# The last 1024 output columns as seven half products, with weight sums built in DRAM

## The chip, the cores and the metric

The kernel runs on one core of a Trainium2 chip. The metric is the device time of one execution in microseconds. A core has a matrix engine (TensorE, PE in the profile), a vector engine (DVE), a scalar engine (ACT), GpSimd (POOL) and a queue engine that issues transfers (SP); 16 DMA engines move the data. Matrix products leave their results in PSUM, in banks of 512 float32 columns per partition.

## The reference

One layer of a hybrid decoder block on 512 rows of 2048 features, in float32. A normalised input is projected to 5120 columns, which feed three groups of heads: a state space model (1024 output features), differential attention (512) and cross attention to a memory (512). Their concatenated outputs go through one square output projection, whose rows are normalised and added to the input:

```python
mix = jnp.concatenate([y_s, y_d, y_x], axis=-1) @ w_out[l]     # (512 x 2048) @ (2048 x 2048)
x = x + rmsnorm(mix, norm_post[l])                             # mean of squares over all 2048 columns of a row
```

The change concerns this product and what follows it. Everything before it stays, but for the shape of two buffers.

## The kernel before, in words

All products are made at float32 precision from two halves of each factor: `split` and `parts` make a rounded copy `hi` (ACT) and the rest `lo` (DVE), and `mm3` multiplies hi by hi, hi by lo and lo by hi, three matmuls into the same PSUM bank.

The matrix engine's work is a list, `chunks`. A chunk is 512 KB of weights, 128 partitions of 1024 numbers, and a function that issues its matmuls in four units. The loop over `chunks` loads the raw weights some chunks ahead (`load`, tile `raw`, two buffers), splits them two chunks ahead (`parts`, tiles `whi` and `wlo`, three buffers each) and runs the units. Vector and scalar work hangs on quarter chunks: `at_slot(n, f)` calls f after a unit of chunk n. Matmuls are kept in the order in which they are written. On the other engines and in SP's queue a planner may put an instruction that is ready ahead of an earlier one that is not; the marks that `parts` leaves keep vector and scalar instructions behind the split before them. Engines work their queues in order.

The stages are: input projection, state space scan (to chunk `S1`), its gate (`w_glu`, `S1` to `S2`), the remaining projections and cross attention (`S2` to `S3`), differential attention (`S3` to `S4`), and from `S4` the output projection. S4 begins at about 617 us.

The output projection has the weights `w_out_b`, in 4 blocks of 512 columns with 8 chunks each; a chunk holds two slabs of 128 rows of the weight matrix and 512 columns. A block takes, in each chunk, 4 row tiles of 128 rows x 2 slabs x 3 matmuls of 512 columns: 24 per chunk, 192 per block. The factor from the left, kept in SBUF as hi and lo, is `ys` (8 slabs, from `out_open`), `yd` (4) and `yx` (4). Blocks 0 to 2 are made by `add_rows`, four banks `ps_mm` for the four row tiles. `out_evac` then takes a bank: ACT sums the squares of its row (`ojk`, sums in `fin["ss"]`), DVE multiplies by the norm's weights `gpost` into `mix`, which stays in SBUF.

Block 3 is cut: its first four chunks run like the others, over five `pieces`: row tiles 0 to 2, and row tile 3 in two halves of 256 columns, the second half in a bank of its own (`ps_s`). The weights of its last four chunks are all split beforehand (`load_last`, tiles `last4` to `last7`), and so the rest runs piece by piece: a row tile is finished, and while the next one is multiplied, its mean of squares is made (DVE, power -1/2 on POOL), and x plus the scaled mix is written out by DVE (`xres`, `xraw`: two instructions of 1024 columns) and stored. Only the second half of row tile 3 has no matmuls to hide behind. x is loaded by `load_last` into its own buffers.

Of the kernel before, what the change touches and what calls it, by code (L numbers as in the profile page):

```python
# [10 lines left out]
F32 = mybir.dt.float32  # L11
# [8 lines left out]
P = 128  # L20
# [34 lines left out]
def tile_hybrid_block(ctx: ExitStack, tc: tile.TileContext, a: dict, out: bass.AP):  # L55
# [39 lines left out]
    def mm(*args, **kw):  # L95
        pin(pe.matmul(*args, **kw))  # L96
# [1 line left out]
    def transpose(o, i):  # L98
        pin(pe.transpose(o, i, ident))  # L99

    def mm3(o, lh, ll, rh, rl, start, stop):
        mm(o, lh, rh, start=start, stop=False)
        mm(o, lh, rl, start=False, stop=False)
        mm(o, ll, rh, start=False, stop=stop)

    def split(hi, lo, x):
        s.copy(hi, x)
        v.tensor_tensor(lo, x, hi, ALU.subtract)

    def load(src, pieces=1, beside=()):  # L110
        raw = wp.tile([P, 1024], F32, tag="raw", name="raw", bufs=2)
# [45 lines left out]
    def rsqrt_mean(dst, ssq, n):  # L157
        v.tensor_scalar(dst, ssq, 1.0 / n, EPS, ALU.mult, ALU.add)
        g.tensor_tensor(dst, dst, neghalf.to_broadcast([P, dst.shape[-1]]), ALU.pow)
# [35 lines left out]
    def at_slot(n, f):  # L195
        side.setdefault(round(4 * n) + 3, []).append(f)
# [550 lines left out]
    S1 = len(chunks)  # L747
    ge = {}
    gestack, xstack, atstack = ExitStack(), ExitStack(), ExitStack()
    yx, yd = [], []  # L750

    def ge_open():
        s5stack.close()
        ydxp = right_pool(ctx, "ydxp")
        for lst, nm in ((yx, "yx"), (yd, "yd")):
            for h in range(4):
                lst.append((ydxp.tile([P, SEQ], F32R, name=f"{nm}hi{h}"), ydxp.tile([P, SEQ], F32R, name=f"{nm}lo{h}")))
# [226 lines left out]


    S4 = len(chunks)
    fin = {}
    ys = []
    order = [6, 7, 0, 1, 2, 3, 4, 5]

    def out_open():
        hp.__exit__(None, None, None)
        ysp = ctx.enter_context(tc.tile_pool(name="ysp", bufs=1, reuse_waits="tile"))
        for j in range(8):
            ys.append((ysp.tile([P, SEQ], F32R, name=f"yshi{j}"), ysp.tile([P, SEQ], F32R, name=f"yslo{j}")))
# [12 lines left out]

    def y_rows(k, ts_):
# [3 lines left out]
    def out_evac(tt, acc, c0, i, then=None):  # L1013
        w = acc.shape[-1]
        jk = fin["p"].tile([P, 512], F32, tag="jk", name="ojk", bufs=2)
        s.activation(jk[:, :w], acc, AF.Square, accum_out=fin["ss"][:, tt, i:i + 1])
        if then:
            then()
        v.tensor_tensor(fin["mix"][tt][:, c0:c0 + w], acc, fin["g"][:, c0:c0 + w], ALU.mult)

    for blk in range(3):
        add_rows(a["w_out_b"][blk], NT, y_rows, order, lambda tt, acc, blk=blk: out_evac(tt, acc, blk * 512, blk))


    pieces = [(tt, c0, w) for tt, c0, w in ((0, 0, 512), (1, 0, 512), (2, 0, 512), (3, 0, 256), (3, 256, 256))]
    lastacc = {}

    def out_piece(i, ci_, wh, wl):
        tt, c0, w = pieces[i]
        if ci_ == 0:  # L1030
            lastacc[i] = psum("mm" if i < 4 else "s")
        for kk in range(2):
            lh, ll = y_rows(2 * order[ci_] + kk, slice(tt * P, (tt + 1) * P))
            sl = slice(kk * 512 + c0, kk * 512 + c0 + w)
            mm3(lastacc[i][:, :w], lh, ll, wh[:, sl], wl[:, sl], ci_ == 0 and kk == 0, ci_ == 7 and kk == 1)

    for ci_ in range(4):
        def f(wh, wl, ci_=ci_):
            for i in range(5):
                out_piece(i, ci_, wh, wl)  # L1040
                if i != 3:
                    yield
        chunks.append((a["w_out_b"][3, order[ci_]], f))
# [4 lines left out]
    def load_last():
        for ci_ in range(4, 8):
            hl = tuple(fin["w"].tile([P, 1024], F32R, name=f"last{ci_}{x}") for x in "hl")  # L1050
            split(*hl, load(a["w_out_b"][3, order[ci_]]))
            last.append(hl)
        for tt in range(NT):
            for i in range(2):
                if tt < 3:
                    xr = fin["p"].tile([P, 1024], F32, tag="xres", name="xres", bufs=4)
                else:
                    xr = wp.tile([P, 1024], F32, tag="raw", name="xraw", bufs=2)
                sy.dma_start(xr, a["x"][tt * P:(tt + 1) * P, i * 1024:(i + 1) * 1024])
                fin["x", tt, i] = xr  # L1060

    at_slot(S4 + 26, load_last)


    for i in range(9):
# [4 lines left out]
    h_pair(2)  # L1070
    sy.dma_start(cst, a["cst"])
    for n, (_, f) in enumerate(chunks):
        while len(raws) <= min(n + 2 if n < 9 else n + 3, len(chunks) - 1):
            raws.append(load(chunks[len(raws)][0]))
        ahead = n + 1 if n < 9 else n + 2
        while len(ready) <= min(ahead, len(chunks) - 1):
            ready.append(parts(raws[len(ready)], mark=n >= 9))
        units = f(*ready[n])
        for i in range(4):
            next(units, None)  # L1080
            for e in side.get(4 * n + i, []):
                e()

    for i, (tt, c0, w) in enumerate(pieces):
        for ci_ in range(4, 8):
            out_piece(i, ci_, *last[ci_ - 4])
        if i == 4:
            pre = fin["p"].tile([P, 1], F32, name="pre")
            v.tensor_reduce(pre, fin["ss"][:, tt, 0:4], AX.X, ALU.add)
            v.tensor_scalar(pre, pre, 1.0 / D, EPS, ALU.mult, ALU.add)  # L1090
        sr = fin["p"].tile([P, 1], F32, tag="sr", name="sr", bufs=4)

        def scale(i=i, tt=tt, sr=sr):
            if i < 3:
                v.tensor_reduce(sr, fin["ss"][:, tt, 0:4], AX.X, ALU.add)
                rsqrt_mean(sr, sr, D)
            else:
                v.tensor_scalar(sr, fin["ss"][:, tt, 4:5], 1.0 / D, pre, ALU.mult, ALU.add)
                g.tensor_tensor(sr, sr, neghalf, ALU.pow)

        out_evac(tt, lastacc[i][:, :w], 1536 + c0, 3 if i < 4 else 4, scale if i != 3 else None)
        if i == 3:
            continue
        widths = (1024, 1024) if i < 3 else (256, 512, 256, 512, 512)
# [93 lines left out]
```

## Time and profile before

| | |
|---|---|
| median of 3 runs | 815.49 us (811.62 to 815.84) |
| the profiled execution, its own time | 815.97 us |
| its span, first to last instruction | 813.9 us |
| granted TensorE clock, mean | 0.994 |
| TensorE busy | 794.4 us, 98% of the span |
| VectorE busy | 545.2 us, 67% |
| ScalarE busy | 358.9 us, 44% |
| GpSimd busy | 28.3 us, 3% |
| bytes moved by DMA | 131.59 MB, 162 GB/s in the mean |

Busy times are of one engine and overlap between engines. A matmul's own duration overlaps with that of the next, so the pace of matmuls is read from the distance of their starts. A row of a group gives total busy time, mean ns of one, and after the bar the idle time of the engine ahead of it with what ended it. Queues of transfers appear as SPq. In a timeline the first number is the start from the beginning of the span, the second the duration.

### The profile page before, as it was taken

What the parts mean: (1) busy time and instruction counts of PE and PEld (TensorE: products, weight loads), DVE (VectorE), ACT (ScalarE), POOL (GpSimd) and SP (SyncE); (2) the same over time, 40 slices, a digit from 0 to 9 for tenths busy, and PEclk for the clock granted to TensorE, in tenths of its full rate; (3) what the DMA queues carried; (4) which work ended last, traced back from release to release, by engine and by line L of the source; (5) the groups of instructions that cost most, each with busy time, mean ns of one, the idle gap of its engine ahead of it and who ended that gap; (6) DMA issues with size and microseconds to landing.
All of it is one profiled execution on the core that took longest, in us unless ns stands there. A gap on an engine that the chain in (4) does not pass through costs nothing.

```text
span 813.9 us, 10924 instructions
## 1 busy us (share of the span) xinstructions
PE 794.4 (98%) x4030; PEld 663.2 (81%) x4030; DVE 545.2 (67%) x1033; ACT 358.9 (44%) x593; POOL 28.3 (3%) x42
## 2 busy tenths in 40 slices
PE   8999999899999999999999999999999999999996
PEld 6877788788878888888888888888888888888885
DVE  4599878648998899847885544668888833232335
ACT  4654433334445545334734533446667532132311
POOL 0000000010000000000000000000100110000000
PEclk9999999999999999999999999999999999999999
DMA  7977767783655555357564322232224345322326
GB/s 245 351 270 255 255 208 243 250 228 89 189 151 158 150 160 159 116 153 272 175 204 166 100 92 91 78 104 78 78 78 141 96 159 175 104 83 99 109 99 258
DMA packets 60357, 131.59 MB, mean 162 GB/s; under 512 B 12688, under 2 KB 26128, under 8 KB 59408
## 3 DMA queue, kind: packets, MB, share of 16 engines
q1 hardware_dynamic: 60304, 130.91, 49.8%
q8 instruction: 31, 0.51, 0.3%
q14 instruction: 22, 0.18, 0.1%
HBM read 109.52 MB, written 21.36 MB: 161 GB/s over the span
## 4 chain that ended last, share of the span: by engine, by line
PE 82%; DVE 8%; DMA 4%; ACT 2%; issue 2%; SPq 1%; POOL 0%; DVEq 0%; POOLq 0%; ACTq 0%
PE ps_mm L96 71%; PE ps_s L96 7%; PE ps_t L96 3%; DMA raw<-in_w_in_a_dram 2%; DVE wlo L71 2%; PE ps_t L99 1%; DVE ra L71 1%; SPq L71 1%; DMA rows<-in_x_dram 1%; DMA par<-in_par_dram 1%; ACT whi L71 1%; DVE sm L71 1%; DVE x L71 1%; ACT cs L71 1%; DVE cs L71 0%
## 5 line engine op out<-in xcount | busy, mean ns | idle before, releaser
L71 DVE TENSOR_TENSOR wlo<-raw,whi 128x1024 fp32r<-128x1024 f32 (+1 forms) x135 | 161.7, 1198 | 155.2 <-ACT whi L71 154.2
L71 ACT CAST whi<-raw 128x1024 fp32r<-128x1024 f32 (+1 forms) x135 | 138.9, 1029 | 258.4 <-PE ps_mm L96 161.4
L96 PE MATMUL ps_mm<-hhi,whi 128*128 128x512 f32 x512 | 203.0, 396 | 2.8 <-DVE ut L71 1.5
L96 PE MATMUL ps_mm<-hlo,whi 128*128 128x512 f32 x512 | 200.6, 392 | 0.8 <-DVE hlo L71 0.8
L96 PE MATMUL ps_mm<-hhi,wlo 128*128 128x512 f32 x512 | 200.2, 391 | 0.0
L96 PEld LDWEIGHTS ps_mm<-hhi,whi 128*128 128x128 f32 x512 | 96.7, 189 | 24.8 <-ACT hhi L71 2.0
L96 PEld LDWEIGHTS ps_mm<-hhi,wlo 128*128 128x128 f32 x512 | 96.6, 189 | 20.7 <-DVE wlo L71 0.2
L96 PEld LDWEIGHTS ps_mm<-hlo,whi 128*128 128x128 f32 x512 | 96.6, 189 | 20.4 <-DVE hlo L71 1.4
L96 PE MATMUL ps_mm<-whi,hhi 128*128 128x512 f32 x128 | 50.0, 390 | 0.0
L96 PE MATMUL ps_mm<-whi,hlo 128*128 128x512 f32 x128 | 49.9, 390 | 0.0
L96 PE MATMUL ps_mm<-wlo,hhi 128*128 128x512 f32 x128 | 49.9, 389 | 0.0
L96 PE MATMUL ps_mm<-whi,yshi 128*128 128x512 f32 (+1 forms) x112 | 43.9, 392 | 0.0
L96 PE MATMUL ps_mm<-wlo,yshi 128*128 128x512 f32 (+1 forms) x112 | 43.3, 387 | 0.0
L96 PE MATMUL ps_mm<-whi,yslo 128*128 128x512 f32 (+1 forms) x112 | 43.3, 386 | 0.0
L96 PEld LDWEIGHTS ps_mm<-whi,hlo 128*128 128x128 f32 x128 | 24.0, 188 | 5.1
L96 PEld LDWEIGHTS ps_mm<-wlo,hhi 128*128 128x128 f32 x128 | 24.0, 188 | 4.8
L96 PEld LDWEIGHTS ps_mm<-whi,hhi 128*128 128x128 f32 x128 | 24.0, 188 | 4.7
L71 DVE TENSOR_TENSOR x<-ra 64x512 f32<-64x512 f32 x32 | 26.3, 822 | 0.8
L71 ACT ACTIVATE pr<-sm,nm 128x128 f32<-128x128 f32 (+3 forms) x32 | 18.0, 564 | 18.8 <-DVE nm L71 18.6
L96 PE MATMUL ps_mm<-gehi,whi 128*128 128x512 f32 x64 | 25.2, 394 | 0.0
L96 PE MATMUL ps_mm<-gehi,wlo 128*128 128x512 f32 x64 | 25.1, 392 | 0.0
L96 PE MATMUL ps_mm<-whi,yxhi 128*128 128x512 f32 (+1 forms) x64 | 24.9, 389 | 0.0
(323 smaller groups left out, 1383.6 us busy)
## 6 DMA issues: line engine op xcount, KB each, us to landing
raw<-in_w_in_a_dram SPq DMA_DIRECT2D x63, 512.0 KB, 3.5
raw<-in_w_out_b_dram SPq DMA_DIRECT2D x32, 512.0 KB, 3.3
raw<-in_w_in_b_dram SPq DMA_DIRECT2D x16, 512.0 KB, 3.3
sp<-sp_dr SPq DMA_DIRECT2D x8, 576.0 KB, 4.6
rows<-in_x_dram SPq DMA_DIRECT2D x4, 1024.0 KB, 7.7
raw<-in_w_kv_a_dram SPq DMA_DIRECT2D x8, 512.0 KB, 3.4
raw<-in_w_kv_b_dram SPq DMA_DIRECT2D x8, 512.0 KB, 4.4
raw<-in_w_glu_a_dram SPq DMA_DIRECT2D x8, 512.0 KB, 4.5
```

The source lines that it names most:

```text
L71: r = f(*args, **kw)
L96: pin(pe.matmul(*args, **kw))
L99: pin(pe.transpose(o, i, ident))
```

## The change

The output matrix's last 1024 columns are seen as 2 x 2 blocks. With Y the left factor (512 x 2048) cut into A11, A21 (rows 0 to 255 and 256 to 511, first 1024 features) and A12, A22 (the last 1024 features), and W the last 1024 columns of the weights cut into four blocks of 1024 x 512, the result needs 8 half products of 256 x 1024 x 512. One level of Strassen's method (in a form with shared sums) makes it from seven: A11, A12 and A22 and four sums of blocks (n1 to n4), each times a block of W or a sum of blocks (t1, T2, T3, T4).

- Blocks 0 and 1 of the output are made as before. Their `mix` goes to DRAM (`mix_dr`, eight stores of 256 KB) and is read back near the end (`load_mix`).
- `sum_steps`: the sums of weight blocks are built in DRAM. For each of four sums and each of its four chunks GpSimd's queue issues a copy of one block's chunk and later a DMA that adds another block's chunk to it: 32 transfers of 512 KB, one every 1.125 chunks from S1 + 1 on. The chunks are then loaded like any weights.
- The sums of blocks of Y are made on chip. `out_open` subtracts rows 256 to 511 of each slab of ys from rows 0 to 255 (`n3f`, 8 DVE instructions of 128x256); `fin_open` splits it to n3; `comb_n24` and `comb_n1` make n2, n4 and n1 in S4 + 7.75 to S4 + 14.75, in halves of 128x1024: two or three DVE additions and a split each.
- From S5 = S4 + 16 on come six products of 4 chunks, in the order A11 times a block, n3 times T3, A12 times a block, n2 times T2, A22 times T4, n1 times t1. A chunk now serves 2 row tiles: 12 matmuls. A11, n2 and n1 go on top of each other in the two banks `ps_t`, n3 and A22 in two banks `ps_mm`, A12 in `ps_s`. At the end of a product ACT copies the partial sum to SBUF (`keep`), or DVE adds the kept one to the bank, and the row sums of squares and the multiplication by `gpost` follow (`c11`, `c21`, `c22` with `out_c`).
- The seventh product, n4, has its four weight chunks split beforehand (`load_last`, into the tiles of ys) and runs as row tile 0, then row tile 1 in two halves of 256 columns, all on the two banks `ps_t`. Residuals (`residual`): row tiles 2 and 3 are written for the time of n4's row tile 0, row tile 0 after it, row tile 1 last.
- Raw weights have two further buffers (`late_raw`, tag nt) for odd chunks after S5, and are loaded up to five chunks ahead. x loads into the tiles of yx and yd, mix into those of n2 and n1, c12 and the kept sums into those of n2, n3 and n3f.

```diff
-        jk = fin["p"].tile([P, 512], F32, tag="jk", name="ojk", bufs=2)
-        v.tensor_tensor(fin["mix"][tt][:, c0:c0 + w], acc, fin["g"][:, c0:c0 + w], ALU.mult)
-    for blk in range(3):
+            v.tensor_tensor(fin["n3f"][:, j], yr[:, 0:256], yr[:, 256:512], ALU.subtract)
...
+    def comb_n24(k):
+        f_ = fin["n3f"][:, k:k + 4]
+        a12, a22 = half2(k)
+        for n, (h_, l_) in (("n2", a22), ("n4", a12)):
+            v.scalar_tensor_tensor(f_, f_, -1.0, h_, ALU.mult, ALU.subtract)
+            v.tensor_tensor(f_, f_, l_, ALU.subtract)
+            split4(fin[n], k, f_)
+            yield
...
+    def sum_steps():
+        for dst, first, second in (("T3", (1, 2), (2, 2)), ("t1", (1, 1), (1, 2)), ("T2", "T3", (1, 1)), ("T4", "T2", (2, 1))):
+            for c in range(4):
+                g.dma_start(sums[dst][c], sums[first][c] if isinstance(first, str) else block(*first, c))
+                yield
+            for c in range(4):
+                g.dma_start(sums[dst][c], block(*second, c), accum_op=ALU.add, max_dma_last_dim=4096)
+                yield
+    for i in range(32):
+        at_slot(S1 + 1 + 1.125 * i, lambda: next(sum_iter))
...
+    def out_evac(tt, acc, blk):
+        square(acc, tt, blk)
+        cs_ = slice(blk * 512, (blk + 1) * 512)
+        mx = fin["p"].tile([P, 512], F32, tag="mx", name="omx", bufs=3)
+        v.tensor_tensor(mx, acc, fin["g"][:, cs_], ALU.mult)
+        sy.dma_start(mix_dr[tt][:, cs_], mx)
+    for blk in range(2):
...
+    def out_c(c_, tt, col, sign=1.0):
+        w = c_.shape[-1]
+        square(c_, tt, 2 if col < 1536 else 3 + (col > 1536))
+        v.scalar_tensor_tensor(c_, c_, sign, fin["g"][:, col:col + w], ALU.mult, ALU.mult)
+    def c22(i, acc):
+        c_ = tile4("ysp", *KC)[:, 2 + i]
+        v.tensor_tensor(c_, acc, fin["pq"][:, 2 + i], ALU.add)
+        out_c(c_, 2 + i, 1536, -1.0)
...
+    product("A11", w_of(1, 1), "t", True, keep(KA, 0))
+    product("n3", s_of("T3"), "mm", True, keep(KA, 1))
+    product("A12", w_of(2, 1), "s", True, c11)
+    product("n2", s_of("T2"), "t", False, keep(KB, 0))
+    product("A22", s_of("T4"), "mm", False, c21)
+    product("n1", s_of("t1"), "t", False, c22)
...
+    for i, tt in enumerate((2, 3, 0, 1)):
+        at_slot(S5 + 20.25 + 0.5 * i, lambda tt=tt: load_x(tt))
+    at_slot(S5 + 19, lambda: load_mix(0))
+    for ci_ in range(4):
+        at_slot(S5 + 18.75 + ci_, lambda ci_=ci_: load_last(ci_))
...
-        while len(raws) <= min(n + 2 if n < 9 else n + 3, len(chunks) - 1):
-            raws.append(load(chunks[len(raws)][0]))
+        while len(raws) <= min(n + 2 if n < 9 else n + 3 if n < S5 - 2 else n + 5, len(chunks) - 1):
+            m = len(raws)
+            raws.append(load(chunks[m][0], raw=late_raw() if m > S5 and m % 2 else None))
...
+    load_mix(1)
+    acc = last_product(0, 0, 512)
+    for tt in (2, 3):
+        residual(tt, row_scale(tt), (1024, 512, 512), (fin["c2"][:, tt - 2], fin["c2"][:, tt]))
+    c12_evac(0, acc, 0)
+    acc = last_product(1, 0, 256)
+    residual(0, row_scale(0), (1024, 512, 512), (fin["m11"][:, 2], c12[:, 0]))
+    c12_evac(1, acc, 0)
+    acc = last_product(1, 256, 256)
+    pre = fin["p"].tile([P, 1], F32, name="pre")
+    v.tensor_reduce(pre, fin["ss"][:, 1, 0:4], AX.X, ALU.add)
+    v.tensor_scalar(pre, pre, 1.0 / D, EPS, ALU.mult, ALU.add)
+    square(acc, 1, 4)
+    sr = fin["p"].tile([P, 1], F32, tag="sr", name="sr", bufs=4)
+    v.tensor_scalar(sr, fin["ss"][:, 1, 4:5], 1.0 / D, pre, ALU.mult, ALU.add)
+    g.tensor_tensor(sr, sr, neghalf, ALU.pow)
+    v.scalar_tensor_tensor(c12[:, 1, 256:], acc, -1.0, fin["g"][:, 1792:], ALU.mult, ALU.mult)
+    residual(1, sr, (256, 256, 512, 512, 512), (fin["m11"][:, 3], c12[:, 1]))
```

More of the change, by code (lines that the diff above doesn't have):

```diff
@@ L108, in split, with load @@
         v.tensor_tensor(lo, x, hi, ALU.subtract)
-    def load(src, pieces=1, beside=()):
-        raw = wp.tile([P, 1024], F32, tag="raw", name="raw", bufs=2)
+    def load(src, pieces=1, beside=(), raw=None):
+        raw = wp.tile([P, 1024], F32, tag="raw", name="raw", bufs=2) if raw is None else raw
         w = 1024 // pieces
@@ L749, in tile_hybrid_block @@
     gestack, xstack, atstack = ExitStack(), ExitStack(), ExitStack()
-    yx, yd = [], []
+    yx, yd, fin = [], [], {}
     def ge_open():
@@ L1025, in tile_hybrid_block @@
[L1025 to L1043, printed above, removed]
+    def square(x, tt, i):
+        jk = fin["p"].tile([P, 512], F32, tag="jk", name="ojk")
+        s.activation(jk[:, :x.shape[-1]], x, AF.Square, accum_out=fin["ss"][:, tt, i:i + 1])
+    mix_dr = [dr.tile([P, 1024], F32, name=f"mix_dr{tt}") for tt in range(NT)]
@@ L1048, in load_last @@
[L1048 to L1060, printed above, removed]
@@ L1062, in tile_hybrid_block, with rows2, plain @@
-    at_slot(S4 + 26, load_last)
+    for i, k in enumerate((0, 4)):
+        it = comb_n24(k)
+        for j in range(2):
+            at_slot(S4 + 7.75 + 4 * i + j, lambda it=it: next(it))
+        it = comb_n1(k)
+        for j in range(2):
+            at_slot(S4 + 9.75 + 4 * i + j, lambda it=it: next(it))
+    S5 = len(chunks)
+    bank = {}
+    def rows2(name):
+        def plain(hl, c0):
+            return lambda k, i: tuple(t_[:, k, c0 + i * P:c0 + (i + 1) * P] for t_ in hl)
+        if name in ("A12", "A22"):
+            c0 = 0 if name == "A12" else 256
+            return lambda k, i: plain(fin["yd" if k < 4 else "yx"], c0)(k % 4, i)
+        return plain(fin["ys"] if name == "A11" else fin[name], 0)
@@ new lines, in product, with f @@
+    def product(name, src, tag, first, then=None):
+        for c in range(4):
+            def f(wh, wl, c=c):
+                lhs = rows2(name)
+                for i in range(2):
+                    if first and c == 0:
+                        bank[tag, i] = psum(tag)
+                    for kk in range(2):
+                        sl = slice(kk * 512, (kk + 1) * 512)
+                        mm3(bank[tag, i], *lhs(2 * c + kk, i), wh[:, sl], wl[:, sl], first and c == 0 and kk == 0,
+                            c == 3 and kk == 1, skip_group_check=not first)
+                    if c == 3 and then:
+                        then(i, bank[tag, i])
+                    yield
+            chunks.append((src(c), f))
@@ new lines, in s_of, with load_last @@
+    def s_of(n):
+        return lambda c: sums[n][c]
+    product("A11", w_of(1, 1), "t", True, keep(KA, 0))
[4 more added lines that the diff above has]
+    product("n1", s_of("t1"), "t", False, c22)
+    last = []
+    def load_last(ci_):
+        if ci_ == 0:
+            fin["last"] = [fin["ysp"].tile([P, 4, 1024], F32R, tag=f"ys{x}", name=f"last{x}") for x in "hl"]
+        hl = tuple(t_[:, ci_] for t_ in fin["last"])
+        split(*hl, load(block(2, 2, ci_)))
+        last.append(hl)
@@ L1082, in tile_hybrid_block, with residual @@
                 e()
[L1084 to L1104, printed above, removed]
+    def residual(tt, sr, widths, c34):
+        cols_of = {0: fin["mix", tt][:, 0:512], 512: fin["mix", tt][:, 512:1024], 1024: c34[0], 1536: c34[1]}
```

107 lines of the change are left out of this document (89 added, 18 removed).

## The prediction

> **What bounds the kernel now.** I read the page's busy times first, then stretches of the last 160 us, the queue of each engine there, and the chain that ended last.
>
> ```profile
> span 813.9 us, 10924 instructions
> ...
> PE 794.4 (98%) x4030; PEld 663.2 (81%) x4030; DVE 545.2 (67%) x1033; ACT 358.9 (44%) x593; POOL 28.3 (3%) x42
> ...
> L96 PE MATMUL ps_mm<-hhi,whi 128*128 128x512 f32 x512 | 203.0, 396 | 2.8 <-DVE ut L71 1.5
> ...
> 713.38 0.60 ACT L71 ACTIVATE ojk<-ps_mm 128x512 f32<-128x512 f32 x1 [0.35 <-PE ps_mm L96]
> 757.57 0.60 ACT L71 ACTIVATE ojk<-ps_mm 128x512 f32<-128x512 f32 x1 [0.35 <-PE ps_mm L96]
> ...
> 784.03 16.65 PE ps_mm L96 x72
> ...
> 803.35 0.28 PE L96 MATMUL ps_s<-last4h,yshi 128*128 128x256 f32 x1
> 806.09 0.28 PE L96 MATMUL ps_s<-last7h,ydlo 128*128 128x256 f32 x1
> ```
>
> TensorE is the bound from end to end, and the chain is matmuls up to the tail. The 396 ns of a matmul is not its price: matmuls overlap. The two ACT rows are the first squares of output blocks 1 and 2, and both stand in the same place of their block, so one block of 192 matmuls takes 757.57 - 713.38 = 44.19 us, or **0.230 us per 512-column matmul**; the 72 matmuls of the chain row give 0.231. The last 24 half-wide ones run from 803.35 to 806.37, spaced (806.09 - 803.35)/23 = 0.119 us. The last matmul ends at 806.37; the other 7.5 us to 813.9 are the tail (square, scale, residual, output).
>
> Vector and scalar engine are nearly free where the change is made, then busier:
>
> ```profile
> 600.00:660.00 60.00, 60.00 (x315) 50.80 (x314) 47.33 (x135) 38.39 (x95) 6.41 (x9) 1.00 0.35 114
> 660.00:717.00 57.00, 57.00 (x255) 46.52 (x254) 17.86 (x22) 16.17 (x27) 1.08 (x2) 1.00 0.43 148
> 717.00:784.00 67.00, 67.00 (x316) 55.72 (x315) 21.08 (x20) 17.84 (x24) 0.00 (x0) 1.00 0.32 111
> ...
> 32.00:36.00 4.00, 4.00 (x19) 3.31 (x18) 1.79 (x3) 3.39 (x5) 0.00 (x0) 1.00 1.02 399
> ```
>
> After the stretch's length: busy us of PE, weight load, DVE, ACT and POOL, then granted clock, DMA share, GB/s. The last row, from the start of the kernel, is the fastest that DMA ran: 399 GB/s.
>
> **The change, part by part.**
>
> *Matmuls removed.* Output blocks 2 and 3 cost 2 x 192 = 384; seven half products cost 7 x 4 chunks x 2 row tiles x 2 x 3 = 336. The 48 that go are worth 48 x 0.230 = **11.1 us**, on the path. PE would end at 795.3. I call T0 the start of the last product: 24 x 0.230 + 48 x 0.119 = 11.2 us before that, 784.1. Everything else can only take from this gain, since the other edits add work and traffic.
>
> *Faster consumption of weights.* Each 512 KB chunk now feeds 12 matmuls, 2.76 us instead of 5.5. That is 190 GB/s, under half of 399. The load has four buffers and must land some 8 us after issue. The split of a chunk costs
>
> ```profile
> L71 DVE TENSOR_TENSOR wlo<-raw,whi 128x1024 fp32r<-128x1024 f32 x25 | 30.6, 1224 | 65.9 <-ACT whi L71 65.9
> L71 ACT CAST whi<-raw 128x1024 fp32r<-128x1024 f32 x25 | 26.2, 1048 | 67.8 <-PE ps_mm L96 63.9 <-PE ps_s L96 3.9
> L71 DVE TENSOR_TENSOR mix<-ps_mm,gpost 128x512 f32<-128x512 f32 x15 | 10.3, 688 | 6.3 <-ACT ojk L71 6.3
> L71 ACT ACTIVATE ojk<-ps_mm 128x512 f32<-128x512 f32 x15 | 9.0, 599 | 27.5 <-PE ps_mm L96 27.5
> L71 DVE SCALAR_TENSOR_TENSOR xres<-mix,sr,xres 128x1024 f32<-128x1024 f32 x6 | 7.4, 1281 | 2.0 <-POOL sr L159 2.0
> L71 DVE SCALAR_TENSOR_TENSOR xraw<-mix,sr,xraw 128x512 f32<-128x512 f32 x3 | 2.1, 743 | 0.0
> ...
> raw<-in_w_out_b_dram SPq DMA_DIRECT2D x32, 512.0 KB, 3.3
> ```
>
> 2.4 us with the handover, and it starts when a buffer comes free, two chunks (5.5 us) ahead: 3 us of slack remain. A combining output adds 0.69 + 0.74 us per row tile on DVE; a kept one is an ACT copy like the 0.60 of ojk. DVE then works 4 x 1.22 + 2 x 1.43 = 7.8 of 11 us per product at most. Hidden; without the 3 us of slack it would cost up to 1 us per chunk.
>
> *Sums of A rows on the chip.* n3f: eight 128x256 subtractions of about 0.41 us (half-wide mix, shown below) = 3.3 us, in the stretch to 660 where DVE is fullest. What covers them is the lead of DVE over PE:
>
> ```profile
> 647.79 0.75 DVE L71 SCALAR_TENSOR_TENSOR pr<-pr,rl 128x512 f32<-128x512 f32 x1
> 653.11 0.60 PE L99 MATMUL ps_t<-cst,pr 128*128 128x128 f32 x4
> ```
>
> PE transposes the last softmax 4.6 us after DVE finished it, so 3.3 us fits. If the lead were gone, all 3.3 us would be paid. The other combinations are about 22 DVE instructions of 1.2 us and eight ACT casts: 27 and 8 us in the 660 to 717 stretch, where DVE has 39 us idle and ACT 41. Nothing.
>
> *Sums of weight blocks.* 16 copies and 16 accumulating DMAs of 512 KB, DRAM to DRAM, issued by POOL from about 365 to 600 us. The trace has no such transfer. Bounds: 3.3 us each, as a weight load, or several times that. T3 is wanted first, about 717, T4 last, about 750; so even 11 us for each of 32 in a row is in time. Each accumulation waits on POOL's queue for its copy, issued four steps (some 29 us) before, so POOL shouldn't stand. What they could delay is weight loads; the cast row above says what slack these have: ACT's waits there are for PE to free a buffer (63.9 us), not for landings. POOL's own work in that time is the scale of the attention rows; a DMA issue ahead of it delays it by a microsecond or so, inside the same 4.6 us lead. I take 0; the other end is a rival below.
>
> *Mix through DRAM, x later.* Blocks 0 and 1 are stored (2.1 MB) and read again. The eight stores stand on SP's queue, each waiting for DVE's mix tile, 1.4 us after the last; weight loads queue behind them, with 8 us to land in. All 4.2 MB of x now load only after product A22 has freed their tiles, from about T0 - 17; before, most went out from 664 on. With 2.1 MB of last weights and 1.05 MB of chunks, 9.4 MB must pass in the 27 us around T0: 24 us at 399 GB/s. It just fits, but SP issues in order (the second half of mix can't go before n1 ends at T0, and what stands behind it waits), and the last weights have two buffers:
>
> ```profile
> 664.07 0.38 SPq L71 DMA_DIRECT2D xres<-in_x_dram  x1
> 670.50 1.37 SPq L71 DMA_DIRECT2D xres<-in_x_dram  x3
> ...
> 772.92 1.05 ACT L71 CAST last5h<-raw 128x1024 fp32r<-128x1024 f32 x1 [3.54 <-DMA raw<-in_w_out_b_dram]
> 775.04 1.05 ACT L71 CAST last6h<-raw 128x1024 fp32r<-128x1024 f32 x1 [1.07 <-DMA raw<-in_w_out_b_dram]
> 778.45 1.05 ACT L71 CAST last7h<-raw 128x1024 fp32r<-128x1024 f32 x1 [2.36 <-DMA raw<-in_w_out_b_dram]
> ```
>
> Each waits for its landing, 5.6 us from issue to split. Alone the fourth would be split at T0 + 2.5, wanted at T0 + 4.1; behind 2 to 4 MB of x and mix (3 to 5 us) at T0 + 5 to + 7. Price 0 to 4 us of PE wait; it hides in the next term while below 2.
>
> *The last stage on DVE.* The wait of the mix tile (total, times, longest), the end of the queues, and the granted clock behind the last matmul (third number from the right):
>
> ```profile
> DVE mix L71 <- ACT ojk L71: 6.3, 9, 0.8
> ...
> 790.39 0.16 DVE L71 TENSOR_REDUCE sr<-oss 128x1 f32<-128x4 f32 x1 [9.63 <-ACT ojk L71]
> 802.96 2.48 DVE L71 SCALAR_TENSOR_TENSOR xres<-mix,sr,xres 128x1024 f32<-128x1024 f32 x2 [0.65 <-POOL sr L159]
> 805.35 0.41 DVE L71 TENSOR_TENSOR mix<-ps_mm,gpost 128x256 f32<-128x256 f32 x1
> ...
> 803.61 0.38 ACT L71 ACTIVATE ojk<-ps_mm 128x256 f32<-128x256 f32 x1 [2.16 <-PE ps_mm L96]
> 806.46 0.38 ACT L71 ACTIVATE ojk<-ps_s 128x256 f32<-128x256 f32 x1 [2.37 <-PE ps_s L96]
> ...
> 808.00:812.00 4.00, 0.00 (x0) 0.00 (x0) 2.71 (x5) 0.00 (x0) 0.00 (x0) 0.85 0.65 230
> 812.00:814.00 2.00, 0.00 (x0) 0.00 (x0) 0.00 (x0) 0.00 (x0) 0.00 (x0) 0.50 0.17 65
> ```
>
> Before, DVE rested for 9.6 us ahead of 790 and had 22 us of PE time (784.03 to 806.37) for three row tiles' residuals. Now four output row tiles are finished in the 11.2 us after T0. From T0 - 1.2, when n1's first bank is done: c22 twice, 2.9; two or three last-weight splits, 3.0; three row scales, 0.9; residuals of tiles 2, 3 and 0 at 1.28 + 2 x 0.74, less their small overlap, 2.65 each, 8.0; c12 evacuations 0.74 and 0.48. Sum 16.0 us, to T0 + 14.8; PE alone would end at T0 + 11.2. So **DVE is late by 3 us or more**, and it holds PE too: the two halves of row tile 1 now share one bank (before: ps_mm and ps_s, two banks). The mix row shows that accesses to a bank take turns here: it waited 6.3 us for ojk, nine times, though it reads only ps_mm and gpost. If the second half's matmuls wait for the first half's evacuation, what queues ahead on DVE is their wait.
>
> In this trace the half-wide evacuation already stands behind a residual: PE finished that piece at 803.6, DVE took it at 805.35. It cost nothing, as the next piece had its own bank. Now there are two orders. If it goes into the 0.65 us hole in which DVE waits for POOL before residual 0, it is done at 14.8 - 2.65 = T0 + 12.15; if behind that residual, at T0 + 14.8. PE then needs 24 x 0.119 = 2.9 us, and the tail 7.5: the end is at T0 + 22.6 or T0 + 25.2, against 18.7 with no wait. I take the hole, since the piece is ready at about T0 + 9. Without the bank wait DVE's lateness alone gives T0 + 21.5.
>
> [...]
>
> The clock is a further price: after its last matmul at 806.37 PE keeps a mean of 0.85 from 808 to 812 and 0.50 after. If the drop is from 1 to 0.5, it came at 810.8, 4.4 us after the work ended. A PE wait longer than that slows the 24 half matmuls, at most by 2.9 us; mine, from T0 + 8.4 to + 12.2, is 3.8 us and stays just below. [...] The trace's 4.4 decides.
>
> *Sum.* 11.1 - 3.9 (T0 + 22.6 instead of 18.7) = 7.2; less 0.5 for the first stumbles of the doubled load rate = 6.7 us. The profiled run took 815.97 with a span of 813.9; the median of the three runs is 815.49 (811.62 to 815.84). From the median: **808.8 us**. Half a per cent, 4 us, is about what a measurement can tell from no change.
>
> **Rivals.**
>
> *Full gain.* If loads come early and DVE's order keeps row tile 1 ahead, only the 11.1 us count: 804.4. For it: 39 of 57 us idle on DVE before 717. Against: that idleness lies before c22, and residuals cannot start earlier. 0.18.
>
> *The last stage holds longer.* The evacuation stands behind residual 0 (T0 + 25.2), the wait from T0 + 8.4 to + 14.8 is 6.4 us, past the clock's 4.4, which adds up to 2.9: T0 + 28, a gain of 1.8; with the clock untouched 4.6. So 811 to 814. For it: the 805.35 row. Against: a hole is there. 0.24.
>
> *Slower: the sums come late.* Place: the load of T3 chunks ahead of product n3. If an accumulating DMA ran at 20 us or more (26 GB/s), the 32 transfers, 16 x 20 + 16 x 4 = 384 us from 365, would end at 749, the latest that T4 may; from there each further microsecond of one costs 16. It is slower than before once it eats 7 us: 20.5 us each. At 22 us each the kernel would take about 840. Nearest row: 3.3 us for a plain load; factor six against it. 0.13.
>
> **How the numbers follow.** Forecast 0.45, full gain 0.18, longer last stage 0.24, sums late 0.13. Faster by over 0.5% (below 811.4): the forecast but 0.03, full gain, and a little of the third: 0.62. Same: the rest of the third and the 0.03: 0.25. Slower: 0.13. The range from 803.8 (full gain and 0.6 for the runs' scatter) to 816 leaves out the late sums and little else; the forecast's own is 806 to 811.
>
> **What would show it.** 336 matmuls spaced 0.230 from about 717 and no PE wait to about 784: the first step right. PE waits named DVE or ACT between the halves of the last row tile, 3 to 4 us: the bank. A whole line of DVE work after T0 with no idleness: its lateness. ACT casts of the last weights waiting for DMA while x lands: the queue. The prediction is wrong if PE waits for weights of the sums, or earlier than 784 at all.

## The result, and the profile after

The changed kernel takes **877.42 us** (median of four executions, 875.67 to 878.72) where the kernel before takes 815.66 us on the same chip: a ratio of 1.077 (95% interval 1.073 to 1.081), 62 us slower. The forecast was 808.8 us, its range ended at 816. The profiled execution took 878.72 us with a span of 877.0.

From its page: the span, busy times, three of the lines that cut the span into 40 slices of 21.9 us (PE's busy tenths, its granted clock, the DMA engines' share), the software queue of GpSimd (packets, MB, share of 16 engines' time) and an issue row (count, KB each, median us to landing).

```profile
span 877.0 us, 10964 instructions
PE 800.0 (91%) x3958; PEld 661.6 (75%) x3958; DVE 591.8 (67%) x1084; ACT 382.3 (44%) x619; POOL 51.4 (6%) x74
PE   5437599998999999999999999999999899999984
PEclk7767889999999999999999999999999999999997
DMA  9999987677735647534756532322213424436695
q0 software_dynamic: 2816, 16.78, 7.4%
T<-in_w_out_b_dram POOLq DMA_DIRECT2D x16, 512.0 KB, 9.5
```

The same row for the first inputs, from the view of transfers:

```profile
xT<-in_xT_dram SPq DMA_DIRECT2D x7, 512.0 KB, 23.1
```

The loss stands in the first five slices, some 600 us ahead of the seven products: PE is busy for 3 to 7 tenths, its clock is at 6 to 8 tenths, and the DMA share is 9 tenths or more. xT takes 23.1 us to land; before, that row said 6.7. GpSimd's queue in the first 110 us shows why:

```profile
1.25 2.18 POOL L1062 DMA_DIRECT2D T<-in_w_out_b_dram  x4 [0.81 <-POOLq L1352]
...
68.88 0.84 POOL L1065 DMA_DIRECT2D T<-in_w_out_b_dram  x1 [1.12 <-DMA T<-T]
101.45 1.04 POOL L159 TENSOR_TENSOR rcol<-rcol,neghalf 128x4 f32<-128x4 f32 x1 [31.73 <-DVE rcol L71]
102.46 2.60 POOL L1065 DMA_DIRECT2D T<-in_w_out_b_dram  x3
```

The sums of weight blocks are not built from 365 to 600 us. The first copy is issued at 1.25 us, and 29 of the 32 transfers are issued by 70 us, while the kernel loads its first inputs and weights. The price of the start, in stretches (after the stretch's length: busy us of PE, weight load, DVE, ACT and POOL, then clock, DMA share, GB/s), first before, then after:

```profile
0.00:100.00 100.00, 92.59 (x427) 74.54 (x428) 75.07 (x193) 50.85 (x72) 1.52 (x7) 0.98 0.78 274
```

```profile
0.00:100.00 100.00, 58.24 (x197) 43.38 (x198) 27.42 (x67) 29.76 (x38) 19.29 (x35) 0.76 0.98 291
```

Its own loads used 0.78 of the DMA engines already; with the burst the share is 0.98, and PE is busy for 58 us instead of 93. The largest wait of PE (total, times, longest), and the tile view of the first matmuls on the memory (count, ns, first and last start), after and then before:

```profile
PE ps_mm L96 <- ACT hhi L71: 36.4, 4, 11.8
```

```profile
L96 PE MATMUL ps_mm<-mhi,whi x64: 277/281/387, 161.8 to 188.4; 128*128 128x256 f32 x64
```

```profile
L96 PE MATMUL ps_mm<-mhi,whi x64: 277/280/388, 106.3 to 132.6; 128*128 128x256 f32 x64
```

They start at 161.8 us; before, at 106.3.

The first starts of six such groups cut every trace of this study into stages. All in us; "end" is the span. The kernel before has no last product, so its column joins two stages.

| trace | start to memory | to `whi,hhi` | to last `hhi,whi` | to S5 | S5 to last product | last product to end |
|---|---|---|---|---|---|---|
| before | 106.3 | 307.2 | 201.4 | 102.5 | 96.5 | (both) |
| after | 161.8 | 308.9 | 201.4 | 109.0 | 66.6 | 29.3 |
| sums in their slots | 102.9 | 309.0 | 209.0 | 106.5 | 65.7 | 29.4 |
| no sums | 103.4 | 307.2 | 201.4 | 108.7 | 66.6 | 29.3 |
| one burst at 380 us | 105.4 | 321.6 | 228.6 | 106.5 | 65.7 | 29.3 |
| n3f later | 105.1 | 307.8 | 209.6 | 104.4 | 65.7 | 29.4 |
| last weights early | 102.9 | 307.7 | 201.6 | 104.0 | 68.6 | 26.9 |
| evacuation first | 103.4 | 307.5 | 201.6 | 103.8 | 70.8 | 24.6 |
| whole row tile | 105.6 | 307.4 | 201.6 | 103.8 | 71.3 | 21.0 |
| last weights earlier | 105.9 | 310.0 | 201.6 | 104.1 | 68.1 | 20.9 |
| scales first | 104.6 | 308.2 | 201.6 | 103.7 | 67.1 | 19.3 |
| 8 sums at the start | 122.1 | 307.3 | 201.7 | 103.8 | 66.2 | 19.5 |
| 16 sums at the start | 135.6 | 305.8 | 201.6 | 104.0 | 70.1 | 19.4 |

The traces scatter where they run the same work: those without sums at the start take 102.9 to 106.3 us in the first stage, those without sums in the second 305.8 to 310.0 there. The profiled executions of the whole row tile and of the last weights earlier are the slowest of their kernels.

After against before: 55.5 us in the first stage, 1.7 in the second (inside that scatter), 6.5 between the last `hhi,whi` and S5, and 0.6 won in the last two together: 63.1, the difference of the spans. So there are three questions: the 55.5 us at the start, the 6.5 us ahead of S5, and the seven half products, which should have won 11.1 us and won 0.6.

The stretch ahead of S5, after. PE waits twice; DVE's n3f stands in its queue waiting for a load, with attention work behind it:

```profile
690.21 0.55 PE L99 MATMUL ps_t<-cst,pr 128*128 128x128 f32 x3 [2.13 <-DVE ydl L71]
697.71 0.39 PE L96 MATMUL ps_s<-kh,q 128*128 128x256 f32 x1 [2.11 <-DVE mx L71]
...
694.16 0.43 DVE L71 TENSOR_TENSOR n3f<-yr 128x256 f32<-128x256 f32 x1 [0.81 <-DMA yr<-ys_dr]
694.50 0.48 DVE L71 TENSOR_SCALAR pr<-pr,rl 128x512 f32<-128x512 f32 x1
```

The end, after. The last product starts at 847.7 us:

```profile
845.76 0.33 SPq L71 DMA_DIRECT2D raw<-in_w_out_b_dram  x1
854.00 1.04 ACT L71 CAST lasth<-raw 128x1024 fp32r<-128x1024 f32 x1 [3.41 <-DMA raw<-in_w_out_b_dram]
855.10 0.50 PE L96 MATMUL ps_t<-lasth,n4h 128*128 128x512 f32 x1 [3.02 <-ACT lasth L71]
857.94 0.80 PE L96 MATMUL ps_t<-lastl,n4h 128*128 128x512 f32 x1 [2.34 <-DVE lastl L71]
...
865.38 0.41 DVE L71 SCALAR_TENSOR_TENSOR c<-ps_t,gpost 128x256 f32<-128x256 f32 x1
865.85 0.39 PE L96 MATMUL ps_t<-lasth,n4h 128*128 128x256 f32 x1 [1.69 <-DVE pre L71]
```

The fourth chunk of last weights is issued at 845.76, behind 2 MB of x, and split at 854. PE waits 3.0 us for its hi and 2.3 for its lo, and waits 1.7 us more between the halves of row tile 1, until DVE has taken the first half from the bank. In between it runs at half clock, 0.50 from 858 to 860:

```profile
854.00:856.00 2.00, 0.50 (x1) 0.19 (x1) 1.34 (x3) 1.04 (x1) 0.54 (x1) 0.90 0.97 373
...
858.00:860.00 2.00, 2.00 (x5) 1.62 (x6) 0.54 (x1) 0.00 (x0) 0.00 (x0) 0.50 0.93 356
```

### The profile page after: what moved, and what is told of

Same layout as the page of the kernel before. It is cut to its first block, busy times and chain, and to the rows that moved or that the text cites. A ratio compares the mean times of both kernels' runs of the same rounds, so it can differ in the third digit from the quotient of the medians.

```text
span 877.0 us, 10964 instructions
## 1 busy us (share of the span) xinstructions
PE 800.0 (91%) x3958; PEld 661.6 (75%) x3958; DVE 591.8 (67%) x1084; ACT 382.3 (44%) x619; POOL 51.4 (6%) x74
## 4 chain that ended last, share of the span: by engine, by line
PE 66%; DMA 16%; DVE 10%; ACT 3%; issue 3%; SPq 2%; POOL 0%; POOLq 0%; DVEq 0%; ACTq 0%
PE ps_mm L96 54%; DMA raw<-in_w_in_a_dram 8%; PE ps_t L96 6%; PE ps_s L96 5%; DVE wlo L71 2%; DMA rows<-in_x_dram 2%; SPq L71 2%; DMA raw<-in_w_kv_b_dram 2%; ACT whi L71 1%; DMA yr<-ys_dr 1%; DVE ra L71 1%; PE ps_t L99 1%; DVE sm L71 1%; DMA par<-in_par_dram 1%; DMA sp<-sp_dr 1%
## 5 line engine op out<-in xcount | busy, mean ns | idle before, releaser
L71 DVE TENSOR_TENSOR wlo<-raw,whi 128x1024 fp32r<-128x1024 f32 (+1 forms) x135 | 161.8, 1199 | 151.2 <-ACT whi L71 150.4
L96 PE MATMUL ps_mm<-hhi,whi 128*128 128x512 f32 x512 | 207.8, 406 | 39.4 <-ACT hhi L71 36.4
L96 PE MATMUL ps_mm<-hlo,whi 128*128 128x512 f32 x512 | 204.4, 399 | 0.0
L96 PE MATMUL ps_mm<-hhi,wlo 128*128 128x512 f32 x512 | 203.3, 397 | 1.2 <-DVE wlo L71 1.2
L96 PEld LDWEIGHTS ps_mm<-hlo,whi 128*128 128x128 f32 x512 | 98.8, 193 | 21.1 <-DVE hlo L71 2.0
L159 POOL TENSOR_TENSOR so<-so,neghalf 128x1 f32<-128x1 f32 x16 | 13.5, 842 | 356.3 <-DVE so L71 324.3
L71 ACT ACTIVATE pr<-sm,nm 128x128 f32<-128x128 f32 (+3 forms) x32 | 18.0, 563 | 20.9 <-DVE nm L71 20.8
L71 DVE SCALAR_TENSOR_TENSOR hlo<-xT,cols,hhi 128x512 fp32r<-128x512 f32 x16 | 11.4, 749 | 22.1 <-ACT hhi L71 22.1
L96 PE MATMUL ps_mm<-whi,ysh 128*128 128x512 f32 x64 | 25.8, 404 | 0.0
L71 DVE TENSOR_TENSOR wlo<-nt,whi 128x1024 fp32r<-128x1024 f32 x12 | 14.7, 1224 | 16.4 <-ACT whi L71 16.4
L96 PE MATMUL ps_mm<-whi,ysl 128*128 128x512 f32 x64 | 25.4, 397 | 0.0
L96 PE MATMUL ps_mm<-wlo,ysh 128*128 128x512 f32 x64 | 25.2, 394 | 0.0
```

The lines of the kernel that those rows point to most:

```text
L71: r = f(*args, **kw)
```

## Experiments

Theory A: the sums hurt by *when* they run. `at_slot` fixes only their place in the text; nothing holds GpSimd's queue there. Theory B: accumulating transfers cost this wherever they run.

**Sums in their slots.** Each transfer is put behind a one-element POOL operation on a tile that DVE writes in the slot:

```diff
+        v.memset(tk, 1.0)
+        sums["gate"] = g.tensor_tensor(tk, tk, neghalf, ALU.pow).ins
-                g.dma_start(sums[dst][c], ...)
+                gated(g.dma_start(sums[dst][c], ...))    # ordered behind sums["gate"]
```

> All 32 DMAs of the weight sums stay, but each is issued by POOL behind a one-element operation that reads a tile DVE writes in that DMA's slot; so they run from about 365 us on instead of from 1 us. Theory A (the sums hurt because they run while the first weights and x are loaded): the 55.5 us lost before the first projection and the 1.7 us up to S4 come back, 877.4 - 57.2 = 820 us (818 to 824), PE's first 100 us are again 92 us busy, and a single accumulation lands within some 12 us. Theory B (accumulating DRAM transfers are slow or block other DMAs wherever they run): weight loads land late from 365 us on, PE waits there, 850 us or more.

**No sums.** The 32 transfers are left out, and all four products that need a sum read a plain block instead, so other columns come out.

```diff
-        return lambda c: sums[n][c]
+        return lambda c: block(*{"T3": (1, 2), "t1": (1, 1), "T2": (2, 2), "T4": (2, 1)}[n], c)
```

> No sums at all: the 32 DMAs are left out and the three products that need sums of weight blocks load plain blocks of w_out instead, so the last 1024 columns are computed from other weights. Loads, matmuls and all other work are the same in number and size. Theory A: within 2 us of the kernel with the sums issued in their slots, about 820 us. Theory B: some 820 us here and far above it there. If neither (the 55 us came from another part, as the tiles' new layout): stays near 877 us.

Measured: 825.17 us in the slots (823.19 to 830.44; 1.016 of before, 1.012 to 1.021), 818.34 without sums (1.007, 1.004 to 1.010). The first stage is back to that of before in both, so **the 55.5 us at the start came from the place in time**; theory B, which wanted 850 us or more in the slots, falls. The second stage, in whose last 30 us the slots begin (the first transfer goes out at 382 us, not 365), is 309.0 in the slots and 307.2 without sums, a difference inside the scatter. The expected 820 was missed by 5 us, and the table says where: the sums in their slots still cost 7.6 us between `whi,hhi` and the last `hhi,whi`. One stretch there, first without sums, then with them:

```profile
420.00:440.00 20.00, 20.00 (x96) 16.72 (x95) 10.34 (x17) 8.35 (x16) 0.00 (x0) 1.00 0.64 212
```

```profile
420.00:440.00 20.00, 16.57 (x66) 12.84 (x65) 7.19 (x11) 5.76 (x7) 4.85 (x6) 0.91 0.83 244
460.00:480.00 20.00, 20.00 (x99) 16.80 (x99) 10.26 (x23) 10.26 (x20) 5.41 (x6) 1.00 0.68 168
```

At 420 the engines were 0.64 in use without the sums, and PE loses 3.4 us; at 460, where they were 0.29, PE loses nothing.

**One burst.** All 32 released by the first slot, `for _ in sum_iter: pass` in it.

> All 32 sum DMAs released together at the first slot, about 365 us. Theory A in its strong form (a burst of this size starves the loads anywhere): the burst takes some 70 us, as it did from 1 to 70 us; weight loads land 15 us or later instead of 3.3, against the 5.5 us that a chunk feeds PE; 835 to 865 us. In its weak form (only the start is open to it, where 78% of DMA was in use already and no load is ahead): 820 to 826 us, as for single slots.

858.88 us in its one execution, as the strong form of theory A says. Its slices:

```profile
PE   8998999999999999999437999999999899999984
DMA  7977678754655553589998423232323425446785
```

PE falls to 4, 3 and 7 tenths where DMA is at 9 and 8. So the start is no special place: the same burst costs 14.4 + 27.2 us (second and third stage against no sums) in the middle.

**8 and 16 sums at the start**, on the best kernel below, the others in slots: how does the loss grow?

> The best kernel so far, and the first 8 of the 32 sum DMAs (those of T3) are again free to be issued at the start of the kernel; the other 24 stay in their slots. The software queue's packets took 7.4% of 877 us in the changed kernel, 65 us of all 16 DMA engines, so 2.0 us for each DMA; the kernel's own transfers use 0.78 of the first 100 us, which leaves some 22 us. Account S (the start has that much DMA time to spare, and only the excess is lost): 8 x 2.0 = 16 us fit, the first memory matmul stays at 103 to 108 us and the time at 806 to 810. Account Q (while the burst lasts, the loads that PE waits for get only a share of the engines): the loss is in proportion, 55.5 x 8/32 = 14 us, first memory matmul at about 118 us, the time at about 820.

> The same with the first 16 (T3 and t1) at the start. Account S: 32 us, 10 us more than there is to spare, first memory matmul at about 115 us, the time at about 817. Account Q: 28 us, first memory matmul at about 132 us, the time at about 834.

The row of the first memory matmul in three traces, none, 8 and 16 at the start:

```profile
L96 PE MATMUL ps_mm<-mhi,whi x64: 278/282/388, 104.6 to 131.6; 128*128 128x256 f32 x64
```

```profile
L96 PE MATMUL ps_mm<-mhi,whi x64: 277/285/388, 122.1 to 149.0; 128*128 128x256 f32 x64
```

```profile
L96 PE MATMUL ps_mm<-mhi,whi x64: 278/282/387, 135.6 to 162.1; 128*128 128x256 f32 x64
```

104.6, 122.1, 135.6, and 161.8 with all 32 in the changed kernel: 17.5, 31.0 and 57.2 us lost, about 2 us for each transfer from the first on (2.2, 1.9 and 1.8 in the mean). The times agree, 821.66 and 836.56 us against 806.61. That is account Q, though 3 us above its 14 and 28; the 22 us of DMA time that the start has to spare did not take up any of it. A transfer's own price on the engines is the same 2.0 us (7.4% of 877 us for 32). That POOL's transfers slow SP's loads shows in the landing of xT, 23.1 us with all 32 at the start instead of 6.7, at a DMA share of 0.98 instead of 0.78.

**n3f later.** On the kernel with sums in their slots. `out_open` no longer touches `yr` for it; in `fin_open`, for each half k of the slabs:

```diff
+            v.tensor_tensor(f_, yh[:, k:k + 4, 0:256], yh[:, k:k + 4, 256:512], ALU.subtract)
+            v.tensor_tensor(f_, f_, yl[:, k:k + 4, 0:256], ALU.add)
+            v.tensor_tensor(f_, f_, yl[:, k:k + 4, 256:512], ALU.subtract)
```

> As the kernel with the sums in their slots, and n3f is no longer computed from the yr tiles in the attention stretch but six slots later from the split parts (six DVE operations of 1.2 us instead of eight of 0.42). Theory C (the eight n3f operations in the full DVE queue hold up the last attention head and cost the 6.7 us between S4 and S5): 6 to 7 us less, about 813.5 us, with no PE wait over 0.5 us between S4 and S5. Rival (the 6.7 us come from the larger loads and other layout of that stretch, or the added 4 us of DVE work make a new wait): 819 to 821 us.

823.23 us (1.013, 1.010 to 1.016), 2 us less than 825.17, not 6 to 7, and the two intervals overlap; so the effect is read from the trace. The stage ahead of S5 fell from 106.5 to 104.4 (108.7 without sums, 109.0 after). The largest wait in it:

```profile
PE ps_mm L96 <- DVE omx L71: 1.7, 1, 1.7
```

The two waits for attention work are gone, as theory C says, and a third has come: the lump of DVE work now stands ahead of the evacuations at the end of a block. Both sides were partly right. Moving n3f took back 2 to 4.6 us of the stage, depending on which of the three traces with the same code there (106.5, 108.7, 109.0) it is held against. These three differ by what PE waited: 2.5 us in the slots, nearly all for `ydl`, and 4.3 without sums and 4.2 after, for `ydl` and `mx`. Each also shows the half clock for about 3.4 us near the end of one of these waits, worth up to 1.7 us: from 639.5 in the slots, from 698.6 to 702.0 after, and without sums within 620 to 640, where a mean of 0.91 makes 3.6 us. In the slots it came and went in these two stretches:

```profile
639.00:640.00 1.00, 1.00 (x7) 0.90 (x8) 1.00 (x3) 1.00 (x2) 0.00 (x0) 0.75 0.92 348
...
642.00:643.00 1.00, 1.00 (x5) 0.81 (x5) 0.77 (x3) 0.62 (x1) 0.46 (x1) 0.54 0.54 182
```

The 102.5 us of before, the waits and the 1.7 make 106.7, 108.5 and 108.4, against 106.5, 108.7 and 109.0. With n3f later the clock is 1.00 in the whole stage (its longest `whi,ysh` product into `ps_mm` takes 0.48 us, against 0.63 in the three), and 102.5 plus 1.9 us of waits make its 104.4. So n3f cost some 4 to 6 us there, and its later place gave 1.9 back.

**Three edits in three stages.**

```diff
-        at_slot(S1 + 1 + 1.125 * i, paced)
+        at_slot(S1 + 11 + 0.9 * i, paced)
+        at_slot(S4 + (6.25, 11.5)[i], lambda k=k: comb_n3(k))
-        at_slot(S5 + 18.75 + ci_, lambda ci_=ci_: load_last(ci_))
+        at_slot(S5 + 6.75 + 3 * ci_, lambda ci_=ci_: load_last(ci_))
```

> Built on the kernel with n3f computed later (823.2 us), three edits that each act in a stage of their own. (1) The sums' slots begin ten chunks later, at about 440 us: the DMA use of the stretch from 365 to 440 was 0.55 to 0.82 without the sums, from 440 to 620 it was 0.25 to 0.33, so the 8 us that the sums still cost between 413 and 521 us go. (2) The n3 work is spread over two slots away from the evacuations at the end of a block: the PE wait of 1.7 us for the mix tile goes. (3) The four last weight chunks are loaded and split from S5 + 6.75 on, three chunks apart, instead of next to the x loads: the 5.3 us of PE waits at the start of the last product go, and so does the halved clock of its second row tile; the wait between the two halves of row tile 1 stays. If the late loads are the cause of the long end, the kernel ends 22 us after the start of the last product instead of 29.4. Sum 823.2 - 8 - 1.7 - 7 = 806.5 us (804 to 810). Rival for the end: DVE's queue of residuals sets it and not the loads; then it stays 27 us or longer and the time is 811 us or more.

813.93 us (1.001, 1.000 to 1.003), not 806.5. (1) came true: 209.6 to 201.6 in the third stage. These rows, before and in the last kernel of this study, show 180 of 180 us of PE under all the sums, with the DMA share up from 0.28 to 0.67:

```profile
440.00:620.00 180.00, 180.00 (x872) 151.36 (x871) 119.60 (x258) 94.84 (x192) 5.48 (x7) 1.00 0.28 93
```

```profile
440.00:620.00 180.00, 180.00 (x871) 151.20 (x870) 119.86 (x288) 95.19 (x192) 45.69 (x67) 1.00 0.67 180
```

(2) is small, 104.4 to 104.0. (3) was half true: PE no longer waits for last weights, but the end is still 26.9 us, as the wait between the halves of row tile 1 grew from 1.7 to 5.0.

**The bank.** Two more kernels, each on top of the one before: the evacuation of row tile 1's first half ahead of most of residual 0, and row tile 1 in one piece of 512 columns.

```diff
+    c12_evac(1, acc, 0)
     residual(0, row_scale(0), ...)
-    c12_evac(1, acc, 0)
```

> As the kernel with the last weights early, and the evacuation of the first half of row tile 1 stands ahead of the two 512-wide parts of residual 0 on DVE instead of behind them. If the second half's matmuls wait for that evacuation (same PSUM bank, other columns), their wait of about 2 us shrinks to below 1 and the time falls by 1 to 1.5 us, to about 805. If the wait is for the scale chain or for DVE's work as a whole, nothing changes.

```diff
-    acc = last_product(1, 0, 256)
-    c12_evac(1, acc, 0)
+    acc = last_product(1, 0, 512)
...
-    acc = last_product(1, 256, 256)
```

> As that, but the last row tile is done in one piece of 512 columns, so no matmul follows an evacuation in its bank. The bank theory: no PE wait at all after the start of the last product, its last matmul ends 11.1 us after its first. The tail grows by the wider square and evacuation, 0.22 + 0.26 us. About 804.5 to 806 us; if the halves' wait was not the bank, 806 to 807.

The wait with the evacuation behind residual 0, and then ahead of its last parts:

```profile
797.85 0.42 DVE L71 SCALAR_TENSOR_TENSOR c<-ps_t,gpost 128x256 f32<-128x256 f32 x1
798.32 0.58 PE L96 MATMUL ps_t<-lasth,n4h 128*128 128x256 f32 x1 [5.03 <-DVE pre L71]
```

```profile
798.78 0.42 DVE L71 SCALAR_TENSOR_TENSOR c<-ps_t,gpost 128x256 f32<-128x256 f32 x1
799.25 0.39 PE L96 MATMUL ps_t<-lasth,n4h 128*128 128x256 f32 x1 [3.71 <-DVE c L71]
```

In both, PE starts 0.05 us after the evacuation ends (797.85 + 0.42 = 798.27, 798.78 + 0.42 = 799.20), though it writes other columns; the trace names `pre` as the releaser in the first, but in the second `pre` only starts at 800.44, after the wait, and the evacuation `c` is named. Releasers are read from semaphores, so this shows that the program holds these matmuls back until the evacuation of the other columns is done; what the two would do without that wait, no run shows. In one piece there is no such wait, and the last product's stage goes from 24.6 to 21.0. Times: 812.23 us (0.999, 0.998 to 1.000) and **809.57 us (0.997, 0.996 to 0.998)**. The first's interval overlaps that of 813.93: the shorter wait alone is not shown to be worth anything. The second is 4.4 and 2.7 us below these two, and the first of these kernels that beats the one before, by 0.3%. The expected 805 was missed because another stage had grown: S5 to the last product took 71.3 us. SP's queue and PE there:

```profile
769.39 0.42 SPq L71 DMA_DIRECT2D xr<-in_x_dram  x1
774.32 0.32 SPq L71 DMA_DIRECT2D raw<-t  x1
774.75 1.33 SPq L71 DMA_DIRECT2D xr<-in_x_dram  x3
...
781.44 0.50 PE L96 MATMUL ps_t<-whi,n1h 128*128 128x512 f32 x1 [1.53 <-ACT whi L71]
```

**Last weights earlier, scales first.** First `S5 + 5.75 + 2.25 * ci_`, then on top of it:

```diff
-        residual(tt, row_scale(tt), ...)          # tt = 2, 3
+    rs = [row_scale(tt) for tt in (2, 3)]
+    residual(2, rs[0], ...)
+    square(acc, 0, 3)
+    rs.append(row_scale(0))
+    residual(3, rs[1], ...)
```

> As the kernel with the whole last row tile (809.6 us), with one number changed: the four last weight chunks are loaded from S5 + 5.75 on, 2.25 chunks apart instead of 3 from 6.75. There the fourth held one of the two raw buffers, so a chunk of product n1 was issued behind the first x load and PE waited for weights from 774 to 783 us, S5 to the last product taking 71.3 us instead of 66. If that is the cause, all n1 chunks are issued ahead of x, the 66 us return and the time falls by 4 to 5 us, to about 805. Rival: DVE has too much to split in that stretch (9 of 11 us per product), then the waits move to A12 or n2 and the time stays 808 to 810.

> As that, and the scale of row tile 3 is computed ahead of the residual of row tile 2, that of row tile 0 ahead of the end of residual 3, so DVE no longer waits 0.65 us for POOL before a residual, twice. After the start of the last product DVE has no rest, so each 0.65 us counts: 1 to 1.3 us less than without, about 804. If the end were set by PE or by the output's DMA, nothing changes.

807.71 us (0.993, 0.991 to 0.996) and **806.61 us (0.9925, 0.990 to 0.995)**, against 812.86 before: the best of the study. Expected were 805 and 804. The loads now stand in the wanted order, from the last kernel:

```profile
770.35 0.32 SPq L71 DMA_DIRECT2D nt<-t  x1
770.72 0.43 SPq L71 DMA_DIRECT2D mixr<-mix_dr  x1
771.20 3.03 SPq L71 DMA_DIRECT2D xr<-in_x_dram  x4
```

S5 to the last product is 68.1 and 67.1 us, and the end 20.9 and 19.3. The two times' intervals overlap, so the worth of the second edit is read from that stage alone: 1.6 us (21.0 and 20.9 in the two traces without it, 19.3 to 19.5 in the three with it). The order of the loads leaves no slack: the kernel with 16 sums at the start has the same code and order there, yet PE waited 1.3 and 0.8 us for weights of n1 and the stage took 70.1.

## Why the prediction was wrong, step by step

*Sums of weight blocks: the step that failed.* The prediction let them be "issued by POOL from about 365 to 600 us" and priced them at 0. The price was right for a free stretch, as the last kernel's 180 of 180 us show; the times were read off `at_slot`. The description of the kernel had it in a sentence: a planner may put a ready instruction ahead of an earlier one, and the marks hold vector and scalar work only. A copy from an input to DRAM waits for nothing: the first was issued at 1.25 us. Cost: 55.5 us in the first stage; the 1.7 of the second is inside the traces' scatter. The reason given for 0 was also read in the wrong place: the 25 casts of that row are those from 618 us on, when the sums were to be over. From 365 to 600 us the trace before has this row, where some waits are for landings:

```profile
L71 ACT CAST whi<-raw 128x1024 fp32r<-128x1024 f32 x39 | 40.8, 1047 | 52.9 <-PE ps_mm L96 23.1 <-issue 22.3 <-DMA raw<-in_w_in_b_dram 4.6
```

At the slots as written a further 7.6 us would have been lost, since the first of them lie where DMA was 0.64 in use. The rival "sums come late" looked for danger at the other end; the sums were done 600 us before they were wanted.

*n3f, priced at 0 because DVE leads PE by 4.6 us.* Wrong by most of 6.5 us: 4.2 of waits and up to 1.7 of half clock. The lead was read where the last softmax is transposed (647.79 and 653.11). PE waited for DVE's `ydl` some 22 us earlier in the stage, and there the trace before has hardly any lead:

```profile
629.43 0.69 DVE L71 TENSOR_TENSOR ydlo<-ps_t,ydhi 128x512 fp32r<-128x512 f32 x1
...
630.75 0.49 PE L99 MATMUL ps_t<-cst,pr 128*128 128x128 f32 x3
```

DVE is done at 630.1, PE goes on at 630.75: 0.6 us. The smallest lead of the stretch counts, not the last. And the price of an operation in a full queue was more than its 0.41 us: n3f also waits for its load at the head of the queue (0.81 us at 694.16).

*Matmuls removed, 11.1 us, and weights at the doubled rate hidden.* Right. S5 to the last product takes 65.7 to 67.1 us undisturbed, predicted 784.1 - 717.4 = 66.7. In the last kernel S5 to the end is 67.1 + 19.3 = 86.4 us against 96.5: 10.1 of the 11.1 are there.

*Last weights behind x.* Right in kind, too small: the fourth was to be split at T0 + 5 to + 7 with 0 to 4 us of waiting, hidden below 2. It was split at 854.0 to 857.9, T0 + 6.3 to + 10.2, the lo behind a residual on DVE, and PE waited 5.4 us.

*The last stage, T0 + 22.6; measured T0 + 29.3.* Against 18.7 with no wait: 5.4 for the last weights, 1.7 for the bank, 0.6 in the tail (8.1 us instead of 7.5), and 2.9 as the rest, of which the half clock from 857.9 to 862.4 makes some 2.2. The bank wait was there at 1.7 us because PE was late itself; with the weights early it was 5.0, longer than the forecast's 3.8, and the hole in front of residual 0 was not taken: the rival "last stage holds longer" happened in that kernel, 26.9 us against its 25.2 to 28. For DVE's lateness without the bank the prediction had T0 + 21.5; the kernel with the whole row tile took 21.0. The mix row behind that wait showed no accesses to different columns of a bank, so that it would come there too was an estimate; these runs show it, 1.7, 5.0 and 3.7 us long.

*The clock.* "The trace's 4.4 decides" was wrong. The mean of 0.90 from 854 to 856 puts the drop at 855.6, 3.5 us after the matmuls stopped at 852.1, with a single one in between.

Had the sums kept their slots, the sum of these terms would still have been 7.6 + 6.5 - 0.6, slower than before by some 13 us, as 825.17 says. The seven products win only with four schedule faults mended.

## What to carry to other kernels

A place in the program's text is not a time: for each new transfer ask what it waits for, and if the answer is "nothing", price it at the start of the kernel, against the loads there. In this kernel such work cost its engine time in full (here 2 us per 512 KB transfer) where PE waits for loads, and nothing where the DMA share was 0.28; read the share of the stretch, not of the kernel. A saving of matmuls is kept only if the last row tile's weights, its bank and the residuals behind it are scheduled again for the shorter stage.

## What the runs showed of the hardware that was not expected

In these traces the granted clock does not fall at a fixed time after the last matmul. Worked out from the mean clock of the stretches: 4.4 us before the change and 3.5 in the changed kernel (above); 3.4 us in the kernel with the last weights early:

```profile
796.00:798.00 2.00, 0.00 (x0) 0.00 (x0) 2.00 (x4) 0.00 (x0) 0.00 (x0) 0.68 0.36 135
```

Its matmuls stopped at 793.3, and a mean of 0.68 puts the drop at 796.7. In the kernel with the evacuation first the clock was still 1.00 after 3.7 us of rest and dropped in the next stretch, at 800.4, with matmuls running again:

```profile
798.00:800.00 2.00, 0.75 (x6) 0.75 (x7) 2.00 (x4) 0.00 (x0) 0.00 (x0) 1.00 0.32 121
800.00:802.00 2.00, 2.00 (x13) 2.00 (x13) 0.74 (x3) 0.00 (x0) 0.00 (x0) 0.61 1.01 387
```

With the sums in their slots a rest of 2.1 us (636.8 to 638.9) was followed by a drop: the stretches shown with n3f put the drop at 639.5 and its end at 642.9. In the changed kernel a rest of the same length, up to 690.2, went without a drop before the next rest (the clock is 1.00 from 690.0 to 698.5).

What repeats in these traces is how long the half clock lasts. Worked out in the same way from stretches of 0.5 us, it is 3.4 us there and in the kernel with the evacuation first (800.4 to 803.8), and 6.8 us, twice that, in the changed kernel (855.6 to 862.4) and with the last weights early (796.7 to 803.5).

Why the drop comes at such different times, and why it lasts one or the other, no run shows. In this kernel rests like these, 2.1 to 5.0 us long, are therefore priced as a possible half clock for 3.4 or 6.8 us, which is an estimate from these traces.
